# Attention kernel: a pair's softmax reciprocals transposed as one 128x8 block and spread over partitions by a transfer from memory, in place of four 128x128 transposes

## The chip, the cores and the metric

One core of a Trainium2 chip runs the whole program. Its engines run beside each other and meet only at semaphores: TensorE (PE) for matmuls and transposes into PSUM, VectorE (DVE), ScalarE (ACT), GpSimd (POOL), and SyncE (SP), which issues most of the DMA transfers in one queue, in order. The metric is the device time of one execution in microseconds, as the median over runs. Lower is better.

## The reference

One layer of a streaming encoder over 2048 frames of width 1024. A shared projection feeds a state-space group (head group A) and chunked attention (head group B, 8 heads of 64). Their normalised outputs go through one output projection, then through a SwiGLU feed-forward block. The change lies in head group B, of which this is the core:

```python
scores = jnp.einsum('bnqhd,bnkhd->bhnqk', qc, kb).astype(jnp.float32) / math.sqrt(HEAD_DIM)
scores = scores + bias[None, :, None, :, :]
scores = jnp.where(valid[None, None, :, None, :], scores, -1e30)
probs = jax.nn.softmax(scores, axis=-1)
out = jnp.einsum('bhnqk,bnkhd->bnqhd', probs.astype(v.dtype), vb)
```

Each frame attends to its own chunk of 64 frames and the 8 chunks before it. The softmax divides by a sum per head and frame. The kernel applies this division last, to the product of the unnormalised weights with the values.

## The kernel before

The program runs as a prologue, the attention stage (some 130 to 680 us of the profile), the mixing stage with the output projection, and the feed-forward block. The state-space work and all projections of head group B are cut into small pieces and woven into the attention stage as filler for TensorE.

The attention stage is a loop over 128 steps. A step is (sb, pr, hh, qp): four blocks of 512 frames (`sb`), four pairs of heads each (`pr`), two heads of a pair (`hh`), four tiles of 128 frames each (`qp`). So a pair takes 8 steps and there are 16 pairs. Let s be the last step of a pair. Each step issues, in the order of the letters in `ORDER` (`s`, `p`, `t`, `f`; another order in three of every 32 steps, but not in the last block):

- `s`, `scores`: score matmuls (names `sc`, line 83) with the queries as weights; VectorE adds the bias and takes the minimum (`mn`, line 963); ScalarE takes the exponential and sums each row into a column of the pair's tile `sm` (128 frames x 2 heads x 4 tiles; line 966).
- `t`, `transp`, for the step two earlier (`LAG`): up to five transposes of the exponentials into the PSUM tile `pt` (line 86); ScalarE rounds them to `pth` (line 982), VectorE takes the rest as `ptl` (line 983).
- `p`, `pv_head`, at steps s+3 (for the second head) and s−1 (for the first): the product with the values into a PSUM tile `pj`, frames along the free dimension, 64 features along the partitions. ScalarE copies one half (line 1006), VectorE adds (line 1007) into the pair's tile `ya`, 128 features x 512 frames.
- `p`, `pv_scale`, at step s+4: the scaling of `ya`, and its store to memory (line 1017), where the mixing stage fetches it.
- `f`: the filler, units of projections (`pf`) and of the state-space work (`pj`, `X`).

The sums have frames on the partitions and `ya` has them along the free dimension, so the reciprocals have to be turned. `pv_head` of the second head takes the reciprocal of `sm` (128x8, line 993), and ScalarE copies it out to `rb`, 128 x 512, each value repeated 64 times (line 995). `pv_scale` transposes the four 128x128 blocks of `rb` into a `pj` tile (line 86 again, a helper's line), and VectorE multiplies `ya` by that (line 1016).

What sets the order: `k.ta` and `k.te` keep TensorE's instructions in the order of the program. For the other engines and the SP queue a planner picks the order when the program is built, from priorities (the order of the program) and its own estimate of when each instruction is ready. An engine runs its queue in order, so an instruction that waits holds up what stands behind it. The tag `pj` has two PSUM buffers, `sc` and `pt` have one each.

Of the kernel before, what the change touches and what calls it, by code (L numbers as in the profile page):

```python
# [13 lines left out]
ALU = mybir.AluOpType  # L14
AX = mybir.AxisListType

P = 128
SEQ, D = 2048, 1024
KT = D // P
DS = 512  # L20
# [5 lines left out]
H, HD = 8, 64  # L26
SB = 512
NSB = SEQ // SB
# [76 lines left out]
def f32(ap):  # L105
    return ap.bitcast(F32)
# [42 lines left out]
def spread(k, te, pb, o, c):  # L149

    for i in range(4):
        te.transpose(pb[:, i * P : (i + 1) * P], o[:, c + i : c + i + 1].to_broadcast([P, P]), k.ident[:])
# [27 lines left out]
def split(k, hi, lo, raw):  # L180
    nc = k.nc
    return nc.scalar.copy(hi, raw), nc.vector.tensor_tensor(lo, raw, f32(hi), op=ALU.subtract)  # L182
# [553 lines left out]
def att_phase(k, ident, S, aw, x0, roots):  # L736

    tc, nc, io, pfs = k.tc, k.nc, k.io, k.pfs
    with ExitStack() as cx:
        hT, vts, qk, keep = {0: tuple(zip(*x0))}, {}, {}, {}  # L740

        def behind(on=True):
            return tc.issue_after(k.least) if on and k.least else nullcontext()
# [241 lines left out]
        def pv_head(st):  # L985
            sb, pr, hh, _ = st
            h = 2 * pr + hh
            pth, ptl = st_head[sb, h].p
            if hh == 0:
                yas[sb, pr] = k.t(aa, "ya", [P, SB])  # L990
            if hh == 1:
                rs = k.t(aa, "rs", [P, 2, 4], bufs=2)
                nc.vector.reciprocal(rs[:], sums[sb, pr][:])
                rb = rbs[sb, pr] = k.t(aa, "rb", [P, 4, 2, HD])
                nc.scalar.copy(rb[:], rs[:].rearrange("p h i -> p i h").unsqueeze(3).to_broadcast([P, 4, 2, HD]))
            ya = yas[sb, pr]
            yp = k.t(psum, "pj", [P, 512], bufs=2)
            kbs = [4] + [kb for kb in (range(5, 8) if sb == 0 else (0, 1, 2, 3, 5, 6, 7))]
            for n, kb in enumerate(kbs):
                a, b = max(0, kb - 4), min(3, kb) + 1  # L1000
                vt = vts[4 * (sb - 1) + kb, h // 4][:, h % 4, :]
                for m, px in ((0, pth), (1, ptl)):
                    k.ta.matmul(yp[:, a * P : b * P], vt, px[:, kb % 5, a:b, :].rearrange("p a b -> p (a b)"),
                                     start=n == 0 and m == 0, stop=n == len(kbs) - 1 and m == 1)
            yt = k.t(aa, "yt", [P, SB])
            nc.scalar.copy(yt[:64], yp[64:128, :])
            nc.vector.tensor_tensor(ya[hh * 64 : hh * 64 + 64, :], yp[0:64, :], yt[:64], op=ALU.add)

        def pv_scale(st):

            sb, pr, _, _ = st
            ya, rb = yas[sb, pr], rbs.pop((sb, pr))
            pb = k.t(psum, "pj", [P, 512], bufs=2)
            for i in range(4):
                k.ta.transpose(pb[:, i * P : (i + 1) * P], rb[:, i].rearrange("p h d -> p (h d)"), ident[:])
            nc.vector.tensor_tensor(ya[:], ya[:], pb[:], op=ALU.mult)
            (nc.gpsimd if (sb, pr) == (NSB - 1, 3) else nc.sync).dma_start(S["ya"][sb, pr * P : (pr + 1) * P, :], ya[:])

        st_head, yas, sums, rbs = {}, {}, {}, {}
        steps = [(sb, pr, hh, qp) for sb in range(NSB) for pr in range(4) for hh in range(2) for qp in range(4)]  # L1020
# [14 lines left out]
        aa = cx.enter_context(tc.tile_pool(name="aa", reuse_waits="tile", bufs=1))  # L1035
# [4 lines left out]
        psum = cx.enter_context(tc.tile_pool(name="aps", bufs=1, space=bass.MemoryType.PSUM, reuse_waits="tile"))  # L1040
# [27 lines left out]
        N = len(steps)  # L1068
        for _ in range(V1ST):
            next(v0)  # L1070
        for s in range(N + LAG + 2):
            if s == FETCH:
                sp.release()
                k.my0 = tc.alloc_tile_pool(name="my0", reuse_waits="tile", bufs=1)
                k.y0 = k.t(k.my0, "y0", [P, 4, L, 128])
                k.ys = [r[:, m * SB : m * SB + SB] for r in (k.t(k.lp, "raw", [P, 1024], bufs=2) for _ in range(2)) for m in range(2)]
            if s == OPEN:
                aw.release()
                mix = mix_phase(k, S, lambda: k.t(pfs, "pf", [P, 512]))
                units += [Unit(islice(mix, MIX_N), MIX_N, GSTART, N + LAG, GSTART - OPEN)]  # L1080
            for o in TURNED.get(s % 32, ORDER) if s < N - 32 else ORDER:
                if o == "s" and s < N:
                    scores(steps[s])
                elif o == "t" and LAG <= s < N + LAG:
                    transp(steps[s - LAG])
                    if s in GELU:
                        y = k.y0[:, GELU.index(s)]
                        tc.keep_in_program_order(nc.scalar.activation(y, y, AF.Gelu_apprx_tanh))
                        nc.gpsimd.tensor_copy(k.ys[GELU.index(s)].rearrange("p (c j) -> p c j", j=L), y[:, :, :64].rearrange("p j c -> p c j"))
                elif o == "p" and LAG + 1 <= s < N + LAG + 1 and steps[s - LAG - 1][3] == 3:  # L1090
                    pv_head(steps[s - LAG - 1])
                elif o == "p" and s >= LAG + 2 and steps[s - LAG - 2][2:] == (1, 3):
                    pv_scale(steps[s - LAG - 2])
                elif o == "f":
                    for u in units[: None if s < GSTART else -1]:
                        u.advance(s)
                    if s >= GSTART:
                        with tc.issue_after(k.low):
                            units[-1].advance(s)
                    if s == GATES[0] - 2:  # L1100
                        wg = [k.t(k.lp, "raw", [P, 1024], bufs=2) for _ in range(2)]
                        for m in range(2):
                            nc.sync.dma_start(wg[m][:].rearrange("p (q n) -> p q n", q=2), io["w_glu"][2 * m * P : (2 * m + 2) * P].rearrange("(q p) n -> p q n", p=P))
                    if s in GATES:
                        q = GATES.index(s)
                        tags = [("xt", XB)] * 2 if q == 3 else [(f"hi{q}", 1), (f"lo{q}", 1)]
                        k.Wg[q] = [k.t(k.lp, n, [P, DS], F32R, bufs=c) for n, c in tags]
                        with behind():
                            split(k, k.Wg[q][0][:], k.Wg[q][1][:], wg[q // 2][:, q % 2 * DS : q % 2 * DS + DS])
            if s == HEADS[0]:  # L1110
                k.G = [k.t(k.lp, "w", [P, 2, 1024], F32R, bufs=WB) for _ in range(2)]
            if s in HEADS:
                f = HEADS.index(s)
                with behind():
                    split(k, *gate_operand(k, f), k.ys[f])
            if s in FETCHES:
                f = FETCHES.index(s)
                nc.sync.dma_start(k.y0[:, f], S["y"][:, f * P : (f + 1) * P, :128].rearrange("j p t -> p j t"))
# [6 lines left out]
def gate_operand(k, f):  # L1125

    fs = slice(f % 2 * SB, f % 2 * SB + SB)
    return k.G[f // 2][:, 0, fs], k.G[f // 2][:, 1, fs]
# [816 lines left out]
def block_kernel(tc, io, phases="pusamf"):  # L1945
    nc = tc.nc
    k = K(tc, io)
    k.ssm_eng = nc.gpsimd
    with ExitStack() as cx:
        dram = cx.enter_context(tc.tile_pool(name="dram", bufs=1, space=bass.MemoryType.DRAM))  # L1950
# [3 lines left out]
        def pp():  # L1954
            return tc.tile_pool(name="psum", bufs=4, space=bass.MemoryType.PSUM, reuse_waits="tile")

        S = {
            "u": k.t(dram, "u", [L, DS, NSB, NC // NSB]), "y": k.t(dram, "y", [L, DS, NC]),
            "ya": k.t(dram, "ya_s", [NSB, DS, SB]), "x1": k.t(dram, "x1", [D, SEQ]),
            "k": k.t(dram, "ks", [2, H, P, SB]), "nb": k.t(dram, "nbs", [H, 768]),  # L1960
            "bst": k.t(dram, "bsts", [4, P, 8 * P]), "v": k.t(dram, "vs", [NPR, 2, 2, NS, 9 * CH]),
            "hc": k.t(dram, "hc", [2, 7, P, 4, 512]), "h": k.t(dram, "hs", [4, P, HALF]), "ws": k.t(dram, "wss", [12, P, 2, 1024]),
            "hq": k.t(dram, "hq", [2, F2, 7, P, 512]), "wc": k.t(dram, "wc", [F2, 7, P, 512]), "wt": k.t(dram, "wt", [4, P, HALF]),
            "wo": k.t(dram, "wos", [4, P, 2, D]), "kt": k.t(dram, "kts", [CH, NG, 2, P]), "tm": k.t(dram, "tms", [P, NG, P]),
        }
        k.psum = None
        k.names = {n: a.tensor.name for n, a in S.items()}
        ident = k.t(cp, "ident", [P, P])
# [84 lines left out]
```

## Time and profile before

| | |
|---|---|
| median of three runs | 2195.66 us (2192.89 to 2197.64) |
| the profiled execution | 2199.9 us, of which 2197.8 us is the span of the core |
| busy share of the span | PE 98%, PEld 83%, DVE 70%, ACT 46%, POOL 17% |
| attention stage | about 130 to 680 us |

In the rows of the profile, PEld is the loading of TensorE's weights, which runs beside PE, and SPq is SyncE's queue. A row names the line of the kernel, the engine, the operation, the output and inputs by the program's names, and the shapes. "L83" and "L86" are the lines of the helpers that issue all ordered matmuls and transposes, so these are told apart by their tiles. A wait is put down to what came last by the profile.

### The profile page before, as it was taken

Reading aid. Unit: us, or ns where it says so; the run is one execution under the profiler, and the core shown is the slowest. Engines: PE = TensorE matmul, PEld = TensorE weight load, DVE = VectorE, ACT = ScalarE, POOL = GpSimd, SP = SyncE. Lnnn points to the kernel's source line nnn. Section 1 sums busy time; section 2 is a strip of 40 time slices with the busy share of each in tenths; the row PEclk is TensorE's granted clock in tenths of the full one; section 3 lists DMA queues with packets and bytes.
Section 4 is the critical chain, followed back from the end, with each engine's and each line's share of the span. In section 5 each row is a group of like instructions: output and inputs, shape, how many; then the busy total and the mean of one; then the engine's idle time right before and its main releaser. Section 6 shows DMA issues by size and latency. Waiting matters only on the chain.

```text
span 2197.8 us, 30153 instructions
## 1 busy us (share of the span) xinstructions
PE 2150.3 (98%) x10606; PEld 1813.8 (83%) x10606; DVE 1535.5 (70%) x2680; ACT 1007.1 (46%) x1697; POOL 377.9 (17%) x849
## 2 busy tenths in 40 slices
PE   8999999999998999999999999999999999999998
PEld 6787788998887888888888888888888878888887
DVE  8767566666567657766776769667665577688785
ACT  6356466655586621533333345333333443354332
POOL 3367767676310000000000000000000100000000
PEclk9999999999999999999999999999999999999999
DMA  9788877965745346834554757555432594465552
GB/s 330 235 284 267 287 231 246 317 209 162 225 137 168 112 144 204 284 108 149 172 187 141 249 198 271 188 181 183 158 121 91 183 363 167 155 226 190 197 215 77
DMA packets 197591, 440.12 MB, mean 200 GB/s; under 512 B 20224, under 2 KB 37680, under 8 KB 190336
## 3 DMA queue, kind: packets, MB, share of 16 engines
q1 hardware_dynamic: 188816, 410.34, 55.9%
q0 software_dynamic: 8624, 27.86, 4.0%
q8 instruction: 83, 1.36, 0.2%
q14 instruction: 68, 0.56, 0.1%
HBM read 294.72 MB, written 135.29 MB: 196 GB/s over the span
## 4 chain that ended last, share of the span: by engine, by line
PE 82%; DVE 5%; POOL 4%; DMA 4%; issue 3%; ACT 2%; SPq 1%; DVEq 0%; ACTq 0%; POOLq 0%
PE X L83 21%; PE ps L83 19%; PE Y L83 11%; PE big L83 9%; PE pf L83 9%; PE W L83 5%; PE pj L83 4%; PE pt L86 2%; PE sc L83 2%; DMA acc<-x 1%; POOL X L647 1%; POOL st L644 1%; POOL X L646 1%; POOL st L645 1%; POOL X L656 1%
## 5 line engine op out<-in xcount | busy, mean ns | idle before, releaser
L83 PE MATMUL X<-hi,c 128*128 128x512 f32 x1408 | 448.9, 389 | 0.0
L83 PE MATMUL ps<-hd,hd 128*128 128x512 f32 (+1 forms) x1920 | 430.5, 386 | 4.7 <-DVE acc L1826 4.7
L83 PEld LDWEIGHTS ps<-hd,hd 128*128 128x128 f32 x1920 | 354.7, 189 | 76.8 <-issue 5.1
L83 PEld LDWEIGHTS X<-hi,c 128*128 128x128 f32 x1408 | 264.2, 188 | 55.2 <-DVE c L182 0.4
L83 PE MATMUL X<-lo,c 128*128 128x512 f32 x704 | 273.9, 389 | 0.0
L182 ACT CAST hd<-hd 128x1536 fp32r<-128x1536 f32 (+2 forms) x114 | 147.8, 1309 | 233.3 <-DMA hd<-hq 182.3
L83 PE MATMUL Y<-hi,c 128*128 128x512 f32 x696 | 222.2, 389 | 0.5 <-DVE u L1624 0.5
L182 DVE TENSOR_TENSOR hd<-hd 128x1536 fp32r<-128x1536 f32 (+2 forms) x114 | 174.8, 1538 | 38.7 <-ACT hd L182 38.2
L182 DVE TENSOR_TENSOR c<-S,c 128x512 fp32r<-128x512 f32 x175 | 120.1, 687 | 98.5 <-ACT c L182 98.3
L1620 ACT COPY u<-X 128x512 f32<-128x512 f32 x132 | 77.4, 586 | 192.0 <-PE X L83 191.9
L83 PE MATMUL big<-m,woh 128*128 128x512 f32 x512 | 161.3, 397 | 0.0
L1826 DVE TENSOR_TENSOR acc<-acc,ps 128x512 f32<-128x512 f32 x196 | 130.4, 681 | 42.8 <-PE ps L83 42.5
L182 ACT CAST c<-S 128x512 fp32r<-128x512 f32 x175 | 108.6, 621 | 106.9 <-PE Y L83 58.2
L83 PEld LDWEIGHTS X<-lo,c 128*128 128x128 f32 x704 | 132.2, 188 | 27.4
L83 PEld LDWEIGHTS Y<-hi,c 128*128 128x128 f32 x696 | 130.6, 188 | 28.0 <-DVE u L1624 0.9
L182 ACT CAST c<-raw 128x512 fp32r<-128x512 f32 x130 | 80.9, 622 | 151.9 <-PE Y L83 74.1
L83 PE MATMUL pf<-hi,w 128*128 128x512 f32 x416 | 147.5, 407 | 0.0
L1804 POOL DMA_DIRECT2D hd<-hq x4 | 2.5, 628 | 811.9 <-PE X L83 811.1
L83 PE MATMUL Y<-lo,c 128*128 128x512 f32 x348 | 135.4, 389 | 0.0
L983 DVE TENSOR_TENSOR ptl<-pt,pth 128x640 fp32r<-128x640 f32 (+3 forms) x152 | 98.0, 645 | 45.8 <-ACT pth L982 41.8
L966 ACT ACTIVATE s<-s,mn 128x640 f32<-128x640 f32 (+4 forms) x128 | 97.9, 765 | 51.4 <-DVE mn L963 48.5
L982 ACT CAST pth<-pt 128x640 fp32r<-128x640 f32 (+3 forms) x152 | 83.7, 550 | 76.2 <-PE pt L86 70.4
(514 smaller groups left out, 4284.6 us busy)
## 6 DMA issues: line engine op xcount, KB each, us to landing
w<-wss SPq DMA_DIRECT2D x36, 1024.0 KB, 6.9
hq<-g SPq DMA_DIRECT2D x140, 256.0 KB, 2.1
hd<-hq SPq DMA_DIRECT2D x35, 768.0 KB, 4.4
hd<-wc SPq DMA_DIRECT2D x35, 768.0 KB, 5.9
raw<-in_w_up SPq DMA_DIRECT2D x44, 512.0 KB, 4.1
raw<-in_w_gate SPq DMA_DIRECT2D x43, 512.0 KB, 3.6
wc<-px SPq DMA_DIRECT2D x66, 256.0 KB, 3.0
wss<-w SPq DMA_DIRECT2D x12, 1024.0 KB, 6.4
```

Source lines behind the costliest of these rows:

```text
L83: return self.tc.keep_in_program_order(self.tc.nc.tensor.matmul(*a, **b))
L86: return self.tc.keep_in_program_order(self.tc.nc.tensor.transpose(*a, **b))
L182: return nc.scalar.copy(hi, raw), nc.vector.tensor_tensor(lo, raw, f32(hi), op=ALU.subtract)
L644: eng.tensor_tensor(t[:, :, :, :n], src, ar, op=ALU.mult)
L645: eng.tensor_tensor(t2[:, :, :, :n], src[:, ::-1], aw, op=ALU.mult)
L646: eng.tensor_tensor(dst, dst, t[:, :, :, :n], op=ALU.add)
L647: eng.tensor_tensor(dst, dst, t2[:, :, :, :n], op=ALU.add)
L966: nc.scalar.activation(s[:, :nk], s[:, :nk], AF.Exp, bias=mn[:], scale=-1.0, accum_out=sums[sb, pr][:, hh, qp : qp + 1])
L982: k.high = nc.scalar.copy(pth[:, a:b, qp, :], pt[:, a:b, :]).ins
L983: k.low = nc.vector.tensor_tensor(ptl[:, a:b, qp, :], pt[:, a:b, :], f32(pth[:, a:b, qp, :]), op=ALU.subtract).ins
L1620: self.kept = nc.scalar.copy(u[:], ps[:]).ins
L1826: V.tensor_tensor(a, a, ps[:], op=ALU.add)
```

## The change

The reciprocals leave `pv_head`, and two new functions are called at the end of a step, after its filler: `recip` at step s+1 and `spread` at step s+2.

`recip` takes the reciprocal of the 128x8 sums, transposes that block once into 8x128 of a `pj` tile, lets ScalarE copy it to the tile `rt`, and stores `rt` to a small buffer in memory (4 KB; two of them in turn). `spread` loads from there, for each head of the pair, the row of its 512 reciprocals into 64 partitions of `rb`, by an access pattern with a step of 0 (two loads of 128 KB). `pv_scale` keeps its place and multiplies `ya` by `rb` in SBUF.

```diff
-            if hh == 1:
-                rs = k.t(aa, "rs", [P, 2, 4], bufs=2)
-                nc.vector.reciprocal(rs[:], sums[sb, pr][:])
-                rb = rbs[sb, pr] = k.t(aa, "rb", [P, 4, 2, HD])
-                nc.scalar.copy(rb[:], rs[:].rearrange("p h i -> p i h").unsqueeze(3).to_broadcast([P, 4, 2, HD]))
...
+        def recip(st):
+
+            sb, pr, _, _ = st
+            rs = k.t(aa, "rs", [P, 2, 4], bufs=2)
+            nc.vector.reciprocal(rs[:], sums[sb, pr][:])
+            pr8 = k.t(psum, "pj", [P, 512], bufs=2)[:8, :P]
+            k.ta.transpose(pr8, rs[:].rearrange("p h i -> p (h i)"), ident[:])
+            rt = k.t(aa, "rt", [8, P])
+            nc.scalar.copy(rt[:], pr8)
+            nc.sync.dma_start(S["rs"][pr % 2], rt[:])
+
+        def spread(st):
+
+            sb, pr, _, _ = st
+            rb = rbs[sb, pr] = k.t(aa, "rb", [P, SB])
+            for hh in range(2):
+                src = S["rs"][pr % 2, hh * 4 : hh * 4 + 4]
+                nc.sync.dma_start(rb[hh * 64 : hh * 64 + 64, :], bass.AP(src.tensor, src.offset, [[0, 64], [1, SB]]))
+
         def pv_scale(st):
...
-            pb = k.t(psum, "pj", [P, 512], bufs=2)
-            for i in range(4):
-                k.ta.transpose(pb[:, i * P : (i + 1) * P], rb[:, i].rearrange("p h d -> p (h d)"), ident[:])
-            nc.vector.tensor_tensor(ya[:], ya[:], pb[:], op=ALU.mult)
+            nc.vector.tensor_tensor(ya[:], ya[:], rb[:], op=ALU.mult)
...
+            for d, do in ((1, recip), (2, spread)):
+                if s >= d and s - d < N and steps[s - d][2:] == (1, 3):
+                    do(steps[s - d])
...
-            "ya": k.t(dram, "ya_s", [NSB, DS, SB]), "x1": k.t(dram, "x1", [D, SEQ]),
+            "ya": k.t(dram, "ya_s", [NSB, DS, SB]), "rs": k.t(dram, "rs_s", [2, 8, P]), "x1": k.t(dram, "x1", [D, SEQ]),
```

## The prediction

> **What bounds the kernel now.** I read the page's head, its busy shares and its chain first.
>
> ```profile
> span 2197.8 us, 30153 instructions
> PE 2150.3 (98%) x10606; PEld 1813.8 (83%) x10606; DVE 1535.5 (70%) x2680; ACT 1007.1 (46%) x1697; POOL 377.9 (17%) x849
> PE 82%; DVE 5%; POOL 4%; DMA 4%; issue 3%; ACT 2%; SPq 1%; DVEq 0%; ACTq 0%; POOLq 0%
> ```
>
> TensorE is the bound of the whole, so an edit is worth what it takes from TensorE's own stream or from its waits. The edit lies in the attention stage alone. The view of busy time by stretches gives that stage:
>
> ```profile
> core 0: us, PE busy (x) PEld busy (x) DVE busy (x) ACT busy (x) POOL busy (x), PEclk, DMA share, GB/s
> 140.00:200.00 60.00, 53.84 (x317) 45.44 (x315) 43.65 (x103) 38.24 (x101) 40.48 (x88) 1.00 0.80 259
> 200.00:300.00 100.00, 94.02 (x533) 81.60 (x532) 60.87 (x126) 56.89 (x135) 75.61 (x175) 0.98 0.89 279
> 300.00:400.00 100.00, 99.12 (x643) 90.75 (x641) 65.14 (x116) 62.23 (x127) 71.06 (x176) 1.00 0.76 243
> 400.00:500.00 100.00, 99.92 (x617) 90.63 (x616) 63.86 (x110) 61.29 (x124) 67.41 (x170) 1.00 0.76 245
> 500.00:600.00 100.00, 95.50 (x580) 85.77 (x579) 59.29 (x101) 54.19 (x107) 44.34 (x98) 0.98 0.61 191
> 600.00:690.00 90.00, 81.65 (x493) 71.42 (x492) 64.68 (x124) 69.53 (x112) 9.28 (x9) 0.96 0.46 151
> ```
>
> From 300 to 500 us TensorE has under 1 us of idle time in 200, so there each TensorE instruction taken out shortens the stage. VectorE and ScalarE are some 60% busy and the DMA engines 60 to 90%. Where TensorE does idle, the view of waits says for whom:
>
> ```profile
> PE pt L86 <- DVE ptl L983: 11.1, 15, 1.3
> PE sc L83 <- DVE mn L963: 6.0, 5, 1.9
> PE pj L83 <- DMA Bst<-bsts: 0.6, 1, 0.6
> ```
>
> It waits mostly for VectorE, which has to empty a PSUM bank, and almost never for a transfer.
>
> **What the change takes out.** Per pair of heads (16 in all) four transposes, one ScalarE copy that spreads the reciprocals, and the PSUM operand of the scaling multiply. The views of the tile and of the line:
>
> ```profile
> L86 PE MATMUL pj<-ident,rb x64: 270/272/296, 168.0 to 677.8; 128*128 128x128 f32 x64
> L995 ACT COPY rb<-rs x16: 601/617/623, 159.0 to 670.5; 128x512 f32<-128x512 f32 x16
> L1016 DVE TENSOR_TENSOR ya<-ya,pj x16: 676/684/689, 171.5 to 685.1; 128x512 f32<-128x512 f32 x16
> ```
>
> The 272 ns of a transpose are its latency. What it costs is the distance to the next start, which the timeline gives (start us, duration us; x4 is four merged instructions):
>
> ```profile
> 590.58 0.31 PE L83 MATMUL sc<-k,q2l 128*128 128x320 f32 x1
> 590.73 0.60 PE L86 MATMUL pj<-ident,rb 128*128 128x128 f32 x4
> 591.17 0.71 PE L86 MATMUL pt<-ident,s 128*128 128x128 f32 x5
> 591.63 0.48 PE L83 MATMUL pf<-hi,w 128*128 128x512 f32 x1
> ```
>
> Four transposes take 591.17 − 590.73 = 0.44 us, 0.11 each; the five behind them 0.46, 0.09 each. The one that stays works on a 128x8 input, but its stream is still 128 columns, so I take 0.11; its bounds are 0.09 (the five) and 0.27 (its whole latency, should nothing overlap it at its new place). Over 16 pairs that is 1.8 us, 1.4 to 4.3.
>
> The 0.44 isn't a gain where the instruction behind the four waits for VectorE anyway. Reading all 16 groups, that is so in four:
>
> ```profile
> 514.06 0.60 PE L86 MATMUL pj<-ident,rb 128*128 128x128 f32 x4
> 515.93 1.33 PE L86 MATMUL pt<-ident,s 128*128 128x128 f32 x5 [1.28 <-DVE ptl L983]
> ...
> 621.64 0.55 PE L86 MATMUL pt<-ident,s 128*128 128x128 f32 x3 [0.37 <-DVE ptl L983]
> ...
> 652.77 0.60 PE L86 MATMUL pj<-ident,rb 128*128 128x128 f32 x4
> 654.41 0.77 PE L86 MATMUL pt<-ident,s 128*128 128x128 f32 x5 [1.05 <-DVE ptl L983]
> 677.44 0.62 PE L86 MATMUL pj<-ident,rb 128*128 128x128 f32 x4
> 684.41 1.19 PE L83 MATMUL big<-w,hi 128*128 128x512 f32 x2 [3.57 <-DVE ya L1250]
> ```
>
> The fourth is the last pair, whose group stands 7 us ahead of a 3.57 us wait. So 12 groups give 12 × 0.44 = 5.3 us and 16 new transposes cost 1.8: a net 3.5 us less (all groups useful: 7.0 − 1.4 = 5.6 less; dear transposes: 5.3 − 4.3 = 1.0 less).
>
> **What it adds on ScalarE and VectorE.** The 617 ns copy becomes a copy of 8x128 out of PSUM. The nearest row is the 128x128 copy:
>
> ```profile
> L982 ACT CAST pth<-pt 128x128 fp32r<-128x128 f32 x37 | 9.7, 262 | 16.4 <-PE pt L86 14.3 <-DVE ptl L983 1.7
> ```
>
> ScalarE loses 0.36 us a pair, 5.7 in all. It lies behind TensorE's stream; I count nothing, with 3/16 of it (the pairs whose group is followed by a wait for ptl), a gain of 1.1, as the other end. The multiply now reads both operands from SBUF. Two groups of that form and size show what this costs:
>
> ```profile
> L815 DVE TENSOR_TENSOR lo<-raw,hi x12: 681/984/1897, 222.2 to 506.8; 128x512 fp32r<-128x512 f32 x12
> L1170 DVE TENSOR_TENSOR sq<-sq,sg x6: 678/679/692, 649.0 to 682.9; 128x512 f32<-128x512 f32 x6
> ```
>
> Before 510 us, with GpSimd 44 to 76% busy, the median is 984 ns; after 649, with GpSimd nearly idle, 679. I take 0.30 us more for the 13 pairs before 600 us: 3.9 us of VectorE. VectorE has 40% idle time to hide this, except where TensorE waits for it; by the same 3/16 it costs the end 0.7 us (0 if hidden, 3.9 if not).
>
> The Trainium skill ("SBUF — State Buffer", "Who interferes with whom") has a rule against this edit: VectorE's second SBUF input comes through a read port that it shares with GpSimd, and the later of the two instructions blocks until the other is done. The trace agrees, by 984 against 679 ns. By that rule each multiply could lose up to one GpSimd instruction, and GpSimd up to one multiply; by the row it is 0.30, and the row goes into the sum.
>
> **What is moved: the division and its transpose.** The transpose now stands at the end of the step after a pair's last scores, ahead of the next score matmuls, and everything behind it on TensorE waits for the division. In most pairs the division already ends 1.4 to 4.8 us before that place. In four it ends later, worst here:
>
> ```profile
> 287.84 0.19 ACT L966 ACTIVATION_READ_ACCUMULATOR s<-s,mn 128x1 f32 x1
> 291.65 0.31 PE L83 MATMUL sc<-k,q2h 128*128 128x320 f32 x1
> 292.32 0.19 DVE L993 RECIPROCAL rs<-sm 128x8 f32<-128x8 f32 x1
> ```
>
> Against a place 0.15 us ahead of that score matmul it would be 1.0 us late, 2.0 over the four. But the sums of this pair are complete at 288.03 us, 3.5 us ahead of that place, and those of the other three 2.6 to 5.1 us ahead; the division was only queued late, since nothing needed it. I take 0, with 2.0 as the other end.
>
> **What is added on the queues.** SP gets three issues a pair, 48 in all: a 4 KB store that waits for ScalarE's copy, and two 128 KB loads that wait for the store to land. While SP waits, the loads queued behind (weights, keys, bias rows) stand. By the waits view TensorE waited for such a load once, 0.6 us, so I count nothing; the other end is one store's landing per late load, 3.6 us. VectorE's multiply now waits for the loads, with ptl and the next score minima queued behind it, and TensorE waits for those. Landing times of like transfers (us from issue; KB; the second line is the store at L1017):
>
> ```profile
> L1017 SPq DMA_DIRECT2D ya_s<-ya x15: 319/387/542, 172.2 to 655.7; - x15
> DMA to landing us min/median/max: 2.2/3.6/6.6
> q2h<-q2h SPq DMA_DIRECT2D x28, 128.0 KB, 4.6
> ```
>
> From the transpose's place: 0.3 us for its result, 0.6 for ScalarE's copy with a short queue, 2.8 for a small store (between 2.2 and 3.6), 0.4 for the first load's issue, 4.6 for the second's landing: 8.7 us. The time there is runs from that place to where the multiply stands now, first and last of 15 pairs (the last pair has more):
>
> ```profile
> 161.69 0.29 PE L83 MATMUL sc<-k,q2h 128*128 128x256 f32 x1
> 171.54 0.68 DVE L1016 TENSOR_TENSOR ya<-ya,pj 128x512 f32<-128x512 f32 x1
> ...
> 645.17 0.31 PE L83 MATMUL sc<-k,q2h 128*128 128x320 f32 x1
> 655.01 0.68 DVE L1016 TENSOR_TENSOR ya<-ya,pj 128x512 f32<-128x512 f32 x1
> ```
>
> That is 10.0 us in both; the 15 read 10.0, 10.2, 12.0, 18.9, 11.9, 10.2, 15.4, 11.5, 11.4, 13.8, 17.0, 11.5, 14.8, 11.0, 10.0. With 8.7 needed none is late, by 1.3 us at least.
>
> **The sum.** −3.5 + 0.7 = −2.8 us, against the profiled execution's 2199.9 us (span 2197.8 and 2.1 around it): 2197.1. That execution is 4.2 us above the median of the runs shown, so on the median's scale the forecast is 2195.7 − 2.8 = 2192.9 us.
>
> **Rivals.** *The spread rows come late (slower).* Place: VectorE at the multiply. If store and loads need 13 us in place of 8.7, the shortfalls of the 15 pairs (13 minus each time above, where positive) sum to 20.3 us. Between none and all of it reaches TensorE; at half it is 10.2 − 2.8, so +7.4 us: 2203. It breaks even near 11.4 us. For it: the DMA share of 0.76 to 0.89 until 500 us, and the 6.6 us that a store at that queue has taken. Against it: the median landings, and the 1.3 us to spare. The Trainium skill ("DMA: Bandwidth & Descriptors", "Anatomy of one DMA") prices a transfer at about 2.0 us plus bytes over 436 GB/s; by an estimate from this, store and load would take 2.0 and 2.3, and this rival would fall. The trace doesn't bear it out: 3.6 us median for 256 KB, where that price gives 2.6.
>
> *Nothing moves.* What TensorE sheds, it waits for ptl instead, as in the four groups above, in all of them: 2195.7. For it: VectorE's longer multiply. Against: 300 to 500 us without idle TensorE time.
>
> *More than the transposes.* The multiply no longer waits for TensorE, ScalarE has 5.7 us less, and the planner puts ptl and the minima earlier. If that takes a third off the 17.1 us of the first two wait rows, it is −2.8 − 5.7: 2187.2. For it: these waits are the stage's only real idle time. Against: none of these waits names the copy or the multiply.
>
> **How the numbers follow.** Forecast 0.45, late rows 0.18, nothing 0.17, more 0.20. What this kernel's measurement can't tell from no change is 0.2%, 4.4 us. The forecast lies inside that, with about a third of its cases beyond it (all groups useful). So faster is 0.20 + 0.16 = 0.36, slower 0.20 (late rows and a little for waits at the new transpose), the same 0.44. The forecast's own range is 2188 to 2196; the range over the cases is 2185 to 2205, which leaves the late rows' far end and a large gain outside.
>
> **What would show it.** Right: 16 pj transposes of about 0.11 us in TensorE's stream, none waiting for rs; no VectorE idle time ahead of the multiply put down to rb's DMA; the multiply near 0.98 us before 500 us and 0.68 after; TensorE's busy time down by about 5 us (48 transposes × 0.11) and the stage by 3. Wrong: VectorE waiting for rb in several pairs, TensorE waiting longer for ptl or mn than the 17 us of now, the division late at the transpose, or weight loads late behind SP's wait for the store.

## The result, and the profile after

The changed kernel takes 2215.11 us (median; 2210.15 to 2220.46), against 2195.14 us for the kernel before. The ratio is 1.0091, with a 95% interval of 1.0076 to 1.0106: 20 us slower (17 to 23). The forecast was 2192.9 us, in a range of 2185 to 2205. Every "us above" or "below" from here on is a ratio to the kernel before in the same comparison, times 2195.

The page of the changed kernel begins so (its profiled execution took 2215.01 us):

```profile
span 2213.0 us, 30147 instructions
PE 2150.2 (97%) x10558; PEld 1810.6 (82%) x10558; DVE 1535.6 (69%) x2680; ACT 1002.3 (45%) x1697; POOL 384.1 (17%) x849
PE 82%; DMA 6%; DVE 6%; issue 2%; ACT 2%; SPq 1%; POOL 0%; DVEq 0%; ACTq 0%
```

TensorE has 48 instructions less (10558 for 10606) and no less busy time (2150.2 us; 2150.3 in the first profile of the kernel before and 2144.4 in a second one). In the chain that ended last, DMA has gone from 4% to 6%. The view by stretches (columns as in the prediction) shows the stage with idle time on TensorE where there was none:

```profile
200.00:300.00 100.00, 91.14 (x501) 77.55 (x500) 58.70 (x124) 53.81 (x131) 70.96 (x167) 0.97 0.87 279
300.00:400.00 100.00, 94.92 (x597) 85.94 (x596) 63.37 (x111) 58.83 (x120) 74.63 (x178) 1.00 0.81 252
400.00:500.00 100.00, 95.31 (x594) 86.32 (x594) 59.76 (x104) 54.54 (x113) 62.13 (x132) 0.98 0.79 244
```

Before, these stretches read 94.02, 99.12 and 99.92. The waits of the attention stage (us in total, times, longest us):

```profile
PE pt L86 <- DVE ptl L983: 18.8, 18, 2.8
DVE ya L1027 <- DMA rb<-rs_s: 13.7, 4, 9.1
PE pj L83 <- DMA Bst<-bsts: 4.1, 1, 4.1
PE pf L83 <- DMA w<-wss: 3.9, 3, 2.1
...
SPq L1013 <- ACT rt L1012: 43.5, 11, 17.1
SPq L1021 <- DMA rs_s<-rt: 21.8, 10, 4.8
```

TensorE's wait for ptl has grown from 11.1 us, that for Bst from 0.6, that for w from nothing (10.4, 1.6 and 1.1 in the second profile of the kernel before). Most of the longer wait for ptl doesn't come from the rows: it is 16.2 us in the first run below, which has no transfers. VectorE waits for the spread rows in four pairs. SP stands 65 us in front of the new store and the new loads.

For the comparison in time I use that second profile, since the first stood 4 us above its median; it took 2195.54 us. Starts of three score minima in it (the fifth step of the third pair, the fifth of the twelfth, and the last step of all):

```profile
203.63 0.29 DVE L963 CUSTOM_DVE_ANT_0 s<-sc,nbb 128x128 f32<-128x128 f32 x1 [4.36 <-PE sc L83]
519.93 0.82 DVE L963 CUSTOM_DVE_ANT_0 s<-sc,nbb 128x640 f32<-128x640 f32 x1 [1.00 <-PE sc L83]
666.62 0.82 DVE L963 CUSTOM_DVE_ANT_0 s<-sc,nbb 128x640 f32<-128x640 f32 x1
```

The same three in the changed kernel:

```profile
209.86 0.28 DVE L963 CUSTOM_DVE_ANT_0 s<-sc,nbb 128x128 f32<-128x128 f32 x1
534.82 0.82 DVE L963 CUSTOM_DVE_ANT_0 s<-sc,nbb 128x640 f32<-128x640 f32 x1 [1.01 <-PE sc L83]
682.26 0.81 DVE L963 CUSTOM_DVE_ANT_0 s<-sc,nbb 128x640 f32<-128x640 f32 x1
```

So 6.2 us are lost by 210 us, 14.9 by 535, 15.6 by the end of the stage, and 19.3 at the end of the program (2213.0 − 2193.7). The last 3.7 us are lost behind the stage, where the change has no instruction; the kernel before's own two profiles differ there by 2.5 us. The first loss is one pair, the second. Its timeline (start us, duration us; several engines in order of time):

```profile
189.16 0.27 PE L86 MATMUL pj<-ident,rs 128*8 128x128 f32 x1
189.47 0.26 ACT L1012 COPY rt<-pj 8x128 f32<-8x128 f32 x1 [0.22 <-PE pj L86]
194.82 0.34 SPq L787 DMA_DIRECT2D xt<-in_xt  x1
196.60 0.47 SPq L606 DMA_DIRECT2D Bst<-bsts  x1
197.12 0.33 SPq L1013 DMA_DIRECT2D rs_s<-rt  x1
199.89 0.28 DVE L983 TENSOR_TENSOR ptl<-pt,pth 128x128 fp32r<-128x128 f32 x1
204.90 2.05 PE L83 MATMUL pj<-hi0x,Bst 128*128 128x256 f32 x4 [4.09 <-DMA Bst<-bsts]
204.99 1.08 SPq L1021 DMA_DIRECT2D rb<-rs_s  x2
209.25 0.69 DVE L1027 TENSOR_TENSOR ya<-ya,rb 128x512 f32<-128x512 f32 x1 [9.07 <-DMA rb<-rs_s]
```

rt is ready at 189.73, but SP issues its store at 197.12: until 194.82 it stands before a load of xt, mostly for that load's buffer, and then four loads go first. The loads of rb wait for the store, which is seen to have landed at 204.99, 7.9 us after its issue began. The rows are there at 209.25, and VectorE has been idle since 200.17. From transpose to multiply the rows took 20.1 us.

The second loss lies at the eighth and ninth pair:

```profile
405.02 0.27 PE L86 MATMUL pj<-ident,rs 128*8 128x128 f32 x1
406.04 0.29 SPq L1013 DMA_DIRECT2D rs_s<-rt  x1
409.79 1.29 SPq L1021 DMA_DIRECT2D rb<-rs_s  x2
418.87 0.69 DVE L1027 TENSOR_TENSOR ya<-ya,rb 128x512 f32<-128x512 f32 x1 [2.42 <-DMA rb<-rs_s]
...
444.24 0.27 PE L86 MATMUL pj<-ident,rs 128*8 128x128 f32 x1 [0.29 <-DVE rs L1008]
457.10 1.29 DVE L1027 TENSOR_TENSOR ya<-ya,rb 128x512 f32<-128x512 f32 x1 [1.58 <-DMA rb<-rs_s]
458.42 0.82 DVE L983 TENSOR_TENSOR ptl<-pt,pth 128x640 fp32r<-128x640 f32 x1
459.30 1.20 PE L86 MATMUL pt<-ident,s 128*128 128x128 f32 x5 [2.76 <-DVE ptl L983]
```

Here the chain takes 13.9 and 12.9 us. In the eighth pair the store leaves at once and is seen to have landed within 3.8 us, but the loads of rb come only 7.8 us after their issue ended (411.08). Ahead of them in the queue went 1 MB of weights, issued at 407.88, which the view of transfers from 405 to 420 us gives a landing of 7.4 us:

```profile
w<-wss SPq DMA_DIRECT2D x1, 1024.0 KB, 7.4
```

The last three rows of the fence above it show how the wait reaches TensorE: the multiply stands in VectorE's queue ahead of ptl, and the transposes into pt wait for ptl, 2.76 us.

### The profile page after: what moved, and what is told of

Same layout as the page of the kernel before. It is cut to its first block, busy times and chain, and to the rows that moved or that the text cites. A ratio compares the mean times of both kernels' runs of the same rounds, so it can differ in the third digit from the quotient of the medians.

```text
span 2213.0 us, 30147 instructions
## 1 busy us (share of the span) xinstructions
PE 2150.2 (97%) x10558; PEld 1810.6 (82%) x10558; DVE 1535.6 (69%) x2680; ACT 1002.3 (45%) x1697; POOL 384.1 (17%) x849
## 4 chain that ended last, share of the span: by engine, by line
PE 82%; DMA 6%; DVE 6%; issue 2%; ACT 2%; SPq 1%; POOL 0%; DVEq 0%; ACTq 0%
PE X L83 21%; PE ps L83 19%; PE Y L83 10%; PE big L83 9%; PE pf L83 9%; PE W L83 5%; PE pj L83 4%; PE pt L86 2%; PE sc L83 2%; DMA acc<-x 1%; DMA rb<-rs_s 1%; DMA w<-wss 1%; DVE ptl L983 1%; DMA nbb<-nbs 1%; DVE w L182 0%
```

## The experiments

Theories: **rows** (VectorE waits for rb), **SP** (the issues and waits of the new transfers delay other loads), and, as the first runs brought it up, **order** (the planner, which sets the order of the queues when the program is built, places other instructions differently) against **given back** (TensorE waits elsewhere for what it sheds). The constant that stands for the reciprocals below is the first column of the gain tile, spread over the free dimension.

**How much the transfers cost: leave them out, leave them unread.** Without transfers:

```diff
-            nc.sync.dma_start(S["rs"][pr % 2], rt[:])
...
-            rb = rbs[sb, pr] = k.t(aa, "rb", [P, SB])
-            for hh in range(2):
-                src = S["rs"][pr % 2, hh * 4 : hh * 4 + 4]
-                nc.sync.dma_start(rb[hh * 64 : hh * 64 + 64, :], bass.AP(src.tensor, src.offset, [[0, 64], [1, SB]]))
+            rbs[sb, pr] = None
...
-            nc.vector.tensor_tensor(ya[:], ya[:], rb[:], op=ALU.mult)
+            nc.vector.tensor_tensor(ya[:], ya[:], k.gm[:, :1].to_broadcast([P, SB]), op=ALU.mult)
```

> The change without its transfers: division, one 128x8 transpose and the small copy stay; store and loads are left out, and the multiply takes a constant per partition (the gain tile) in place of the reciprocals, so the division by the sums is missing from the output. Theory SP (SP stands at the store and at the loads, and the loads behind it come late): 2190 to 2196 us, no wait of TensorE for w or Bst above 1 us. Theory rows (VectorE waits for the spread rows, and TensorE for VectorE): also 2190 to 2196, waits for ptl back from 18.8 to about 11 us. Theory plan (the planner's other order of ScalarE and VectorE costs the time, whatever the transfers do): 2205 to 2215.

Measured: 2202.74 us, ratio 1.0038 (1.0025 to 1.0051), 8.3 us above the kernel before. With store and loads in place and only the multiply's operand changed:

> The change with all its transfers, but nothing reads the spread rows: the multiply takes a constant per partition, so the division by the sums is missing from the output. TensorE's order is that of the change. Theory rows: VectorE's 13.7 us of waits for rb are gone, and with them the longer waits for ptl: 2200 to 2205 us. Theory SP: the waits for w and Bst (8.0 us) stay, 2207 to 2213. Both at work in the shares that the trace shows: about 2207.

Measured: 2205.58 us, 1.0054 (1.0039 to 1.0069), 11.9 us above. So of the 20 us some 8 come with reading the rows, 3.6 with transfers that nobody reads, and 8.3 stay without any transfer. The intervals of these three are about 3 us each way, so the 3.6 alone isn't clear of noise; but TensorE waits 5.3 us for w in the run with unread transfers, and 0.2 us in the run without any.

The traces part this more sharply by place. The first matmul behind the attention stage starts, in the second profile of the kernel before, without transfers, with unread rows and in the changed kernel, at:

```profile
682.77 1.19 PE L83 MATMUL big<-w,hi 128*128 128x512 f32 x2 [3.61 <-DVE ya L1250]
682.73 0.70 PE L83 MATMUL big<-w,hi 128*128 128x512 f32 x2 [4.00 <-DVE ya L1260]
688.90 1.19 PE L83 MATMUL big<-w,hi 128*128 128x512 f32 x2 [3.99 <-DVE ya L1264]
698.35 1.12 PE L83 MATMUL big<-w,hi 128*128 128x512 f32 x2 [3.99 <-DVE ya L1264]
```

In these profiles the transfers thus make the whole of the stage's 15.6 us: 6.2 unread, 9.4 more when read. Without transfers the stage isn't longer at all; that run's 5.6 us (span 2199.3) are lost behind it. The granted clock goes with that: added up over stretches of 10 us from 680 us on, 10.2 us of clock are lost, against 5.1 in the second profile of the kernel before (its first profile lost 10.2 too, and took 2.5 us more there). Over the timed runs, (1 − granted clock) × span is 15.0 us on average without transfers, against 9.9 for the kernel before beside it: some 5 of the 8.3 us. Why more clock is lost in that run isn't settled.

**When the rows are needed and from where the store is issued.** First the multiply one step later, at s+5 (`steps[s - LAG - 3]` for `steps[s - LAG - 2]`):

> The change with the multiply one step (about 4 us) later, at s+5 in place of s+4, except for the last pair. Theory rows: 9 of the 13.7 us of VectorE's waits go (all but the longest, 9.1 us, which shrinks to about 5): 2204 to 2209 us. Theory SP: nothing changes ahead of the multiply, 2211 to 2217.

Measured: 2211.89 us, 1.0078 (1.0061 to 1.0095), 17 us above; VectorE still waits 14.3 us for rb. But the planner hardly followed the edit: in the trace the multiply stands behind as many score minima as in the changed kernel in 15 of 16 pairs. So this run doesn't show what a later multiply would bring. Then the store from ScalarE's queue:

```diff
-            nc.sync.dma_start(S["rs"][pr % 2], rt[:])
+            nc.scalar.dma_start(S["rs"][pr % 2], rt[:])
```

> The change with the 4 KB store issued by ScalarE, right behind its own copy, in place of SP; TensorE's order is that of the change. Theory SP: SP's 43.5 us of waits for rt are gone, the loads behind come in time and the rows earlier: 2198 to 2206 us. Theory rows: the rows come some us earlier, VectorE's waits for rb shrink, the waits for w and Bst stay: 2205 to 2210.

Measured: 2216.27 us, 1.0099 (1.0084 to 1.0114). The second pair and the eighth in its timeline:

```profile
188.92 0.27 ACTq L1013 DMA_DIRECT2D rs_s<-rt  x1
198.17 1.71 SPq L1021 DMA_DIRECT2D rb<-rs_s  x2
207.23 0.68 DVE L1027 TENSOR_TENSOR ya<-ya,rb 128x512 f32<-128x512 f32 x1
...
419.11 0.69 DVE L1027 TENSOR_TENSOR ya<-ya,rb 128x512 f32<-128x512 f32 x1 [4.45 <-DMA rb<-rs_s]
```

The store leaves at once, and the second pair's wait of 9.07 us is gone, though there the planner also put the multiply one score minimum later; the eighth pair's, at the same place, is longer, 4.45 for 2.42 us. Nothing is won in total. SP still stands, now 50.0 us before the loads that wait for the store, so the run refutes only that the store's turn in SP's queue is the whole cause.

**The multiply's place in VectorE's queue.** In the first runs the planner put the multiply ahead of a score minimum behind which it had stood before. The next two hold it behind, the first of them without transfers and with the constant in place of `rb`:

```diff
-            nc.vector.tensor_tensor(ya[:], ya[:], rb[:], op=ALU.mult)
+            with tc.issue_after(k.least):
+                nc.vector.tensor_tensor(ya[:], ya[:], rb[:], op=ALU.mult)
```

> The changed kernel without store and loads, the multiply by a constant of SBUF (as in the first experiment, which was 8.2 us over the kernel before), but with the multiply held behind the score minimum of its step in VectorE's queue, where the kernel before has it in the last three blocks of 512 frames. Theory 'place in VectorE's queue': the 8.2 us go, the time is within 3 us of the kernel before or below it. Theory 'SBUF operand beside GpSimd' (0.3 us and more per multiply): the time stays 4 to 8 us above. Theory 'the division's and transpose's new place': it stays 8 us above.

Measured: 2203.05 us, 1.0035 (1.0023 to 1.0048), 7.7 us above.

> The changed kernel whole, with the multiply held behind the score minimum of its step in VectorE's queue. Theory 'place in VectorE's queue': the minimum no longer stands behind a multiply that waits for rb, and the waits for rb shrink since the multiply comes some 2 us later: 5 to 8 us above the kernel before, in place of 20. Theory 'rows late wherever the multiply stands' (the ptl behind it is held instead): 14 to 20 us above. Theory 'transfers collide' (late weight and bias loads): 14 us or more above, with waits for w and Bst as in the changed kernel (3.9 and 4.1 us).

Measured: 2214.03 us, 1.0087 (1.0069 to 1.0106), 19 us above, with 12.6 us of waits for rb. In these two traces that moves the multiply in four pairs and, with the transfers, in two (the fifth and the thirteenth); in the other waiting pairs it stood behind that minimum already. So the place of the multiply explains neither: that theory fell.

**Are the transposes worth anything?** One transpose in place of four, its block read four times by the multiply, the rest as before; ahead of it, the second profile of the kernel before.

```diff
-            for i in range(4):
-                k.ta.transpose(pb[:, i * P : (i + 1) * P], rb[:, i].rearrange("p h d -> p (h d)"), ident[:])
-            nc.vector.tensor_tensor(ya[:], ya[:], pb[:], op=ALU.mult)
+            k.ta.transpose(pb[:, :P], rb[:, 0].rearrange("p h d -> p (h d)"), ident[:])
+            y4 = ya[:].rearrange("p (i q) -> p i q", i=4)
+            nc.vector.tensor_tensor(y4, y4, pb[:, :P].unsqueeze(1).to_broadcast([P, 4, P]), op=ALU.mult)
```

> The kernel before once more, for a second profile: the first profiled execution (2199.9 us) stood 4 to 5 us above this kernel's own median. Every theory expects the same waits of TensorE in the attention stage (pt for ptl about 11 us, sc for mn about 6) and a span of 2192 to 2198 us.

Measured: 2195.54 us (span 2193.7).

> The kernel before with three of the four transposes of each pair left out: the first one's 128x128 block is read four times over from PSUM by the multiply, so that head and tile get wrong reciprocals in three blocks of four. The division, ScalarE's copy, VectorE's order and the multiply's PSUM operand stay as before. Theory 'the saved transposes are worth their starts': 12 groups of 16 are useful, 3 x 0.11 us each, so 4.0 us less than the kernel before. Theory 'TensorE gives it back' (it waits for ptl or runs at a lower clock instead): no change, within 1.5 us.

Measured: 2195.32 us, 1.0006 (0.9994 to 1.0019). No gain, though 36 useful transposes were gone. Its order differs from before only on ScalarE (the exponential one place later in eight pairs) and SP. With ScalarE's order put back as well:

> As the run with one transpose of four (three blocks of four get wrong reciprocals), with ScalarE's order also that of the kernel before: in eight pairs the planner had put the exponential one place later, behind the rounding copy of pt, and here it is held ahead of it. TensorE's other instructions, VectorE's, ScalarE's and GpSimd's orders are those of before. Theory 'the order gives the transposes' time back': 3 to 5 us below the kernel before. Theory 'TensorE's time is given back whatever the order' (to the waits for ptl and the half-clock stretches): within 1.5 us of it.

Measured: 2197.57 us, 1.0011 (1.0002 to 1.0020). Without any transpose, with the exponential in its old place and then in its new one:

> The kernel before without any of the four transposes, but with the division and ScalarE's spreading copy, which nothing reads; the multiply takes a constant of SBUF and stands behind the minimum; the exponential is held ahead of the rounding copy as in the kernel before. Theory 'the order gives the time back': 4 to 7 us below the kernel before. Theory 'given back whatever the order': within 2 us.

Measured: 2196.83 us, 1.0013 (1.0003 to 1.0023).

> As the run before this one, but with the exponential where the planner puts it (in eight pairs one place later, behind the rounding copy). Theory 'the order gives the time back': 0 to 3 us above the kernel before, and 4 us or more above the run before this one. Theory 'whatever the order': no difference between the two.

Measured: 2198.06 us, 1.0015 (1.0006 to 1.0023). No difference shows between the two places of the exponential, and taking the transposes out makes the kernel 1 to 3 us slower, not 4 to 7 us faster. Much of where the time goes is seen in the waits. In the second profile of the kernel before:

```profile
PE pt L86 <- DVE ptl L983: 10.4, 16, 1.0
```

With one transpose of four, and with none and the old order:

```profile
PE pt L86 <- DVE ptl L983: 13.1, 19, 1.3
```

```profile
PE pt L86 <- DVE ptl L984: 16.6, 20, 2.1
```

The wait grows by 2.7 and by 6.2 us (by 4.5 and 5.3 in the other two of the four runs), where 48 and 64 transposes at 0.11 us are 5.3 and 7.0. pt has one PSUM buffer: TensorE comes to it sooner and finds it full. What the wait doesn't take shortens the stage: with one transpose of four, the first matmul behind it starts 3.8 us sooner than in the second profile of the kernel before (682.77),

```profile
679.02 1.19 PE L83 MATMUL big<-w,hi 128*128 128x512 f32 x2 [3.92 <-DVE ya L1250]
```

and in the other three 0.2 to 1.8 us sooner. But three of the four take 2.8 to 4.2 us more behind the stage, in code that they don't touch, and over the timed runs each of the four loses 1.7 to 2.8 us more clock than the kernel before beside it. So the time is given back in two places, to the waits for ptl and behind the stage; why the clock is lost there isn't settled.

**The rest of the 8 us.** The next runs part the operand from the place of division and transpose. All work of the change left out:

> The kernel before without any division, spreading copy or transpose; the multiply takes a constant of SBUF. It leaves out all of the work that the change touches, so it bounds what the transposes can be worth. By the sum of the prediction: 16 x 0.44 = 7.0 us less, 5.3 for the useful groups alone. By the run with one transpose of four (no change for three quarters of them): within 2 us. If the SBUF operand costs: 5 to 8 us above.

Measured: 2198.92 us, 1.0016 (1.0005 to 1.0026), 3.5 us above. Division and 128x8 transpose back at the old place:

> No store, no loads, the multiply by a constant of SBUF, and division, 128x8 transpose and ScalarE's copy put right ahead of the multiply (the time and place of the four transposes before). Against the run with the multiply behind the minimum (7.8 us above the kernel before), only the place of division and transpose is back. Theory 'the new place costs' (TensorE waits for the division and for the buffer there): within 3 us of the kernel before. Theory 'the SBUF operand costs': still 6 to 9 us above.

Measured: 2200.71 us, 1.0024 (1.0014 to 1.0033), 5.3 us above. At the new place, but with the operand in PSUM:

> Division and 128x8 transpose at the changed kernel's new place, no store and no loads; the multiply reads a constant block from PSUM, which one 128x128 transpose of the identity makes at the old place of the four. Against the run with the multiply behind the minimum (7.8 us above), the operand is back in PSUM and one transpose of a pair is added. Theory 'the SBUF operand costs': within 3 us of the kernel before. Theory 'the new place costs': 6 to 9 us above.

Measured: 2200.28 us, 1.0020 (1.0010 to 1.0030), 4.4 us above. These last two lie between the expectations, so they alone decide nothing. Then each of the two put into the kernel before. The operand:

> The kernel before with all four transposes, the division and the spreading copy in place, but nothing reads their product: the multiply takes a constant of SBUF and stands behind the score minimum of its step in VectorE's queue. TensorE's and SP's orders are those of before, ScalarE's nearly. Theory 'the SBUF operand and the earlier multiply cost': 4 to 6 us above the kernel before, as in the run without any reciprocals. Theory 'the rest of the reordering costs': within 2 us of the kernel before.

Measured: 2196.23 us, 1.0002 (0.9990 to 1.0014): the SBUF operand costs nothing that can be measured. The place, with all old work kept:

> The kernel before whole, with the changed kernel's division, 128x8 transpose and small ScalarE copy added at their new place, where nothing reads them. SP's order is that of before. Theory 'the new place costs' (TensorE waits there for the division and a buffer): 4 to 7 us above the kernel before, of which 1.8 are the 16 added transposes. Theory 'the operand costs, the place doesn't': 2 us above at most.

Measured: 2197.23 us, 1.0013 (1.0000 to 1.0025), 2.9 us above, of which 1.8 would be the added transposes at 0.11 us. So without transfers the parts are 2.9 us for transposes that bring nothing, up to 2.9 for the new place and none for the operand; measured together, 7.7 to 8.3. The difference of some 2 us is inside the intervals; I don't call it explained. Nor does the attention stage alone hold them: on average 15.0, 14.8 and 14.5 us of clock are lost in the runs at 8.3, 7.7 and 5.3 us above, and 10.8 and 10.5 in the last two, about as much as in the kernel before.

**Where the rows are late.** The change in the last eight pairs only:

> The change made in the last 8 of the 16 pairs only; the first 8 are scaled as in the kernel before. In the changed kernel's trace the stage falls back 6.5 us by step 60 (pairs 1 to 8) and 7.7 more by step 92. Theory 'rows late only where the DMA engines are busiest' (0.8 to 0.9 until 300 us): 0 to 4 us above the kernel before. Theory 'rows late by SP's queue wherever weights are loaded': 8 to 11 us above, with waits of VectorE for rb at about 419 and 457 us.

Measured: 2202.16 us, 1.0030 (1.0016 to 1.0043), 6.6 us above, between the two theories. The wait expected at 419 us belongs to the eighth pair, which this run leaves as before, so the upper range counted one late pair too many. Its ninth pair:

```profile
446.91 0.83 DVE L1038 TENSOR_TENSOR ya<-ya,rb 128x512 f32<-128x512 f32 x1 [3.14 <-DMA rb<-rs_s]
```

So the late rows aren't a matter of the first crowded 300 us alone. Last, the chain cut: the loads read rows that are in memory from the start.

```diff
-                src = S["rs"][pr % 2, hh * 4 : hh * 4 + 4]
+                src = io["x"][hh * 4 : hh * 4 + 4, :SB]
```

> The changed kernel whole, but the two loads of a pair read rows of the input, which lie in memory from the start, so that they needn't wait for the store; the multiply still reads what they bring (another factor than the reciprocals). Theory 'the chain of store and loads in SP's queue makes the rows late': no wait of VectorE for rb, and the time falls from 20 us above the kernel before to the 11 of the run whose rows nobody read. Theory 'the loads are late by themselves, behind other traffic': waits for rb of 8 us or more stay, and the time is 17 to 21 us above.

Measured: 2211.07 us, 1.0068 (1.0044 to 1.0091), 15 us above. The waits for rb that are left:

```profile
206.07 0.69 DVE L1027 TENSOR_TENSOR ya<-ya,rb 128x512 f32<-128x512 f32 x1 [6.57 <-DMA rb<-in_x]
415.66 0.69 DVE L1027 TENSOR_TENSOR ya<-ya,rb 128x512 f32<-128x512 f32 x1 [2.15 <-DMA rb<-in_x]
```

This lies between the two theories. Cutting the chain takes 13.7 us of waits to 8.7: the waits of the fifth and ninth pair vanish (in the fifth the planner now issues the loads ahead of the store) and 2.5 us of the second pair's go. There 6.6 stay, because the loads still stand in SP's queue behind the held load of xt, and then 2.0 us for another load (Vm), and are issued at 200.71; in the eighth pair 2.2 stay, where the loads are issued behind w. So both are causes: the store's landing, and a queue that stands or is full of other bytes when their turn comes. No run gave the loads a queue of their own.

## Why the prediction was wrong

The forecast was 2.8 us below the kernel before, the result 20 above. Of these 23 us, some 8 come with rows that are read late, 3.6 with the transfers themselves, and 11 stand between the forecast and the run without transfers: a gain that didn't come, up to 2.9 us for the new place of the transpose, and lost clock, for which the prediction had no term.

- *Net 3.5 us for the transposes.* Failed. One new transpose costs what was taken: in the first pair the second score matmul behind it starts 0.23 us after it (161.89 after 161.66), where in the second profile of the kernel before the two start 0.12 us apart: 0.11. But taking three or four out brought nothing (1 to 3 us the other way in four runs, each give or take 2 to 3 us). The step from "under 1 us of idle time" to "each TensorE instruction taken out shortens the stage" failed: of 5.3 to 7.0 us taken out, 2.7 to 6.2 came back as waits for ptl, in the ring of pt, ScalarE's rounding copy and VectorE's ptl, and what the stage gained (0.2 to 3.8 us) didn't reach the end. For this part the rival "nothing moves" came nearest, and it named the wait.
- *ScalarE's copy, 262 ns, counted at nothing.* Right: its median is 255 ns, and no run shows a gain from less work on ScalarE (3.5 us above without the 617 ns copy, 2.9 and 3.3 with it).
- *The multiply, 0.30 us more.* Mis-sized. Its row in the changed kernel:

```profile
L1027 DVE TENSOR_TENSOR ya<-ya,rb x16: 679/693/1290, 179.5 to 698.9; 128x512 f32<-128x512 f32 x16
```

  The median is 693 ns for 684 before, three reach 1.0 to 1.3 us; the mean by the groups is 801, so 0.12 us more. Put into the kernel before, an SBUF operand costs 0.4 us in all (−2 to +3). The Trainium skill ("SBUF — State Buffer", "Who interferes with whom") has the rule that the prediction names. The longest multiply agrees with it: it starts at 457.10 us and takes 1.29 us beside a GpSimd instruction that had begun before it,

```profile
456.79 1.05 POOL L655 TENSOR_TENSOR fx<-X,a 128x434 f32<-128x434 f32 x1
```

  but only three of the 16 were held up so much.
- *Division and transpose moved, 0 with 2.0 as the other end.* Not refuted: 2.9 us (0 to 5.5) with the added transposes in it, and one of the 16 waited 0.29 us for the division (444.24).
- *48 issues on SP counted at nothing.* Failed: TensorE's waits for Bst and w are 3.5 and 3.9 us longer than in the first profile (2.5 and 2.8 than in the second), and unread transfers cost 3.6 us (0 or 7 within the noise; 6.2 at the end of the stage in the profiles). Why Bst is late with read rows and on time with unread ones (a wait of 1.1 us) isn't settled. The prediction asked what stands behind SP's wait for the store. It didn't ask what SP stands before when the store's turn comes.
- *The rows need 8.7 us and have 10.0.* Failed, and this is the largest single term. In the four waiting pairs (second, fifth, eighth, ninth) they needed 20.1, 9.4 (296.43 to 305.78), 13.9 and 12.9 us. Three parts of the sum were wrong: nothing was put in for the store's turn in SP's queue (7.4 us in the second pair), its landing was taken as 2.8 us (7.9 there, 3.8 at most in the eighth), and that of the second load as 4.6 (7.8 in the eighth). The fifth pair waited only 0.6 us, because VectorE came to the multiply 8.8 us after the transpose, where 11.9 had been read. In the other pairs VectorE didn't wait: the late ones are those that weren't like the median on which the sum rests. The price that the prediction cites from the Trainium skill ("DMA: Bandwidth & Descriptors", "Anatomy of one DMA") is a fit on transfers issued by GpSimd; the second pair's store, issued by SP, took 7.9 us where that price gives 2.0. The rival of late rows named the place, VectorE at the multiply, and gave 2203 us at 13 us; it was held to be 0.18 likely. Of 13.7 us of waits about 8 reach the end (the changed kernel against unread transfers), somewhat more than the half that it assumed. Its mechanism was right; its size was partly luck, since it summed 20.3 us over ten pairs, where 13.7 us fell on four.
- *Lost clock: no term.* Failed by leaving it out: about 6 of the 20 us (below).
- What was to show it wrong did: VectorE waiting for rb, TensorE for ptl alone 18.8 us, loads late behind SP. What was to show it right held for the 16 transposes' cost, and for the multiply after 500 us (0.68 to 0.69 us). It failed for the multiply before 500 us (a median of about 0.75, not 0.98) and for the stage, which became 15.6 us longer; TensorE's busy time didn't fall by 5 us.

The Trainium skill ("DMA: Bandwidth & Descriptors", "Queues, rings and completion order") says that SP has one ring on each DMA engine, that what stands in a ring is taken in its order, and that transfers need not complete in the order of issue. Here the small store was issued right behind Bst. In the changed kernel the two are seen to have landed within 0.1 us (204.90 and 204.99); with unread rows the store is seen landed at 200.75, 0.95 us before Bst (201.70). So being issued behind Bst doesn't by itself make the store land behind it. No run tests the order in a ring by itself.

## What to carry to other kernels

A small transfer that must pass through a queue shared with bulk loads costs its turn in that queue first: read, for each instance, where that queue stands at that moment, not only the median landing. An engine that is 99% busy isn't thereby the only bound: before an instruction's time is counted as a gain, look for the one-buffer ring that the next instruction waits on, and try it by leaving the work out. Mark in each profile where the changed stage ends: what is lost behind it isn't the edit's own work, and here it was lost clock. And see in the trace whether an edit of the order reached the engine's queue before reading its time.

## What the runs showed of the hardware

A gap costs more than its length. In the changed kernel the matmuls behind the 4.09 us wait for Bst ran slow (ns min/median/max of the tile view, and the stretch by the view of windows, whose third number from the end is the granted clock):

```profile
L83 PE MATMUL pj<-lo0x,Bst x4: 634/634/634, 206.7 to 208.0; 128*128 128x256 f32 x4
```

```profile
200.00:210.00 10.00, 5.91 (x19) 4.66 (x18) 0.93 (x3) 2.74 (x8) 0.00 (x0) 0.67 0.65 187
```

The same in the first profile of the kernel before:

```profile
L83 PE MATMUL pj<-lo0x,Bst x4: 379/379/379, 201.8 to 202.5; 128*128 128x256 f32 x4
```

```profile
200.00:210.00 10.00, 9.35 (x49) 8.05 (x48) 4.54 (x11) 6.04 (x17) 4.52 (x8) 1.00 1.02 365
```

Cut into stretches of 10 us, nearly all others have a clock of 1.00, and the low ones cluster at 0.83 and 0.66 or add up to it with a neighbour: the clock is lost in portions of 1.7 us. The same place of one kernel can lose it or not: from 720 to 730 us the kernel before has 0.87 in its first profile and 1.00 in its second, with the same gap of 0.25 us ahead. Slow matmuls also keep TensorE's busy time up: it is 2150.2, 2150.3 and 2144.4 us in the changed kernel and the two profiles of the kernel before, where the stretches add up to 17.1, 13.6 and 6.8 us of lost clock. (1 − clock) × span, as a mean over the timed runs, is 10.3 us for the kernel before, 16.6 for the changed one, 12.0 to 13.0 for the four runs with fewer transposes, and 21.0 for the store from ScalarE. So 6 of the 20 us are clock, as far as TensorE bounds those stretches, and 4 to 5 of them are lost without any transfer as well (15.0 and 14.8 in the two such runs with the new place of the transpose). The Trainium skill ("TensorE: Matmul & The Clock Gate", "Part 1: The HAM clock gate (the "warmup" mystery)") has a half rate, switched by free-running windows of 3.4 us. By an estimate from that, one window at half rate loses 1.7 us, and the rows agree.
